# Score matmuls of sliding-window attention: 64 queries against 192 keys in place of 128 against 256

## The chip, the cores and the metric

The kernel runs on one core of a Trainium2 chip. The metric is the time of one execution in microseconds on the device, as the median of several runs. TensorE (PE in the profile) multiplies matrices, with weight loads (PEld) as instructions of their own; VectorE (DVE), ScalarE (ACT) and GpSimd (POOL) work on tiles in on-chip memory; SyncE (SP) issues most of the transfers.

## The reference

One layer of a decoder trunk for 1024 prompt tokens and 8 x 4 decode tokens. The part that matters here is the attention of the prompt: 8 query heads of 64 channels share 2 key heads, and a query sees the 128 newest keys including its own, with a learned sink in the softmax's denominator. The reference works in blocks of 128 queries and takes 256 keys for each, the block before and the block itself; the mask leaves 128 of them.

```python
a = jnp.arange(WINDOW)[:, None]
c = jnp.arange(2 * WINDOW)[None, :]
d = a + WINDOW - c
mask = (d >= 0)[None] & (d < WINDOW)[None] & (blk * WINDOW + c[None] - WINDOW >= 0)
...
s = jnp.einsum('bnqhgd,bnkhd->bnhgqk', q, k).astype(jnp.float32) * (HEAD_DIM ** -0.5)
s = jnp.where(mask[None, :, None, None], s, -jnp.inf)
m = jnp.maximum(jnp.max(s, axis=-1, keepdims=True), sink)
p = jnp.exp(s - m)
denom = jnp.sum(p, axis=-1, keepdims=True) + jnp.exp(sink - m)
w = (p / denom).astype(v.dtype)
return jnp.einsum('bnhgqk,bnkhd->bnqhgd', w, v)
```

Around it stand an RMS norm, one input projection, a pooling mixer, an output projection, a SwiGLU FFN and a gated per-layer input.

## The kernel before, in words

All activations lie with channels on partitions. The 1056 tokens are cut into three groups of 352. Most of the time goes into the projections and the FFN, whose weights are split into a high and a low part (L173 casts on ScalarE, L174 subtracts on VectorE), with three matmuls of one pass for each product. The attention's own matmuls are in full fp32, and each of them has two records in the profile. All matmuls go through the helper at L128, all transposes through the one at L122.

The eight blocks of the prompt are worked through in the order 6, 7, 5, 0, 1, 2, 3, 4. A step of the loop issues, in this order: `scores` of the next block, one `filler` (a projection's matmuls, 12 or 24 of 352 columns), `turned` of the current block, another `filler`, and `values` of the current block. The scores of blocks 6 and 7 are issued ahead of the loop, among the decode tokens' attention. TensorE keeps this written order throughout. On VectorE and ScalarE the framework's scheduler decides the order, except where `fix` pins an instruction.

`scores(b)` multiplies, for each pair of heads c and each key head kv, the 128 queries of the block (weights of 64 rows, 128 columns) with 256 keys; kv 0 lies on the lower 64 rows and kv 1 on the upper. Four PSUM banks hold the result, two heads each. Query q of a block sees the key in column c of the block before where c > q, and column c of its own block where c <= q, so exactly one of the two blocks counts for each c. The kernel packs them into a tile `t` of 128 columns a head: ScalarE copies the previous block's 128 scores (L749), and VectorE's predicated copy (L750) puts the own block's scores over them where the mask says so. Block 0 has no block before it; its scores get a mask added instead (L752).

`weigh` is the softmax over the packed tile, once for each key head: maximum (L696), scale and sink (L698, L700), the exponentials with their sums on ScalarE (L707), the denominator (L712, L713), and the division on GpSimd (L715). `turned` transposes the weights, four heads into a bank, and VectorE multiplies each bank with two masks (L771 for the part that belongs to the own block or to the mixed tile `vmix`, L773 for the rest). `values` multiplies these with the value tiles: four matmuls of 128 rows x 64 columns that need the L771 products, and four of 64 x 64 that need those of L773. `put` splits the result into high and low parts (L686, L687).

The fillers bring their own work to the other engines: L856, L875, L877, L885 and L862 to L866 evict, add and square the projections' results.

Of the kernel before, what the change touches and what calls it, by code (L numbers as in the profile page):

```python
# [16 lines left out]
P = 128  # L17
# [14 lines left out]
WIN = 128  # L32
# [13 lines left out]
NEG = -1.0e30  # L46
# [16 lines left out]
def trunk_kernel(  # L63
# [33 lines left out]
    te, ve, se, ge = nc.tensor, nc.vector, nc.scalar, nc.gpsimd  # L97
# [10 lines left out]
    def nm(s):  # L108
        cnt[0] += 1
        return f"{s}{cnt[0]}"  # L110

    def act_tile(shape, dt=F32, s="a"):
        return apool.tile(shape, dt, tag="a", bufs=A_SLOTS, name=nm(s))
# [12 lines left out]
    def mm(*args, **kw):  # L126

        ins = te.matmul(*args, **kw)  # L128
        if pinned[0]:
            tc.keep_in_program_order(ins)  # L130

    def bank():
        return psum.tile([P, 512], F32, tag="b", name=nm("b"))
# [363 lines left out]
    n = 4 * NDEC * PST  # L497
# [141 lines left out]
    kT, vT, qT = qkv[0], qkv[1], qkv[2:]  # L639
# [5 lines left out]
    qd, am, vdec = misc[:, 0, :], misc[:, 1:5, :], misc[: NDEC * DSEQ, 5, :]  # L645
    for c in range(4):
        n = NDEC * DSEQ
# [69 lines left out]
    def m4(i):  # L717
        return am[:, i, :].unsqueeze(1).to_broadcast([P, 4, WIN])
# [4 lines left out]
    def scores(b, now_=True):  # L723


        t = act_tile([P, 8, WIN])
        nk = 2 * WIN if b else WIN
        lo = b * WIN + WIN - nk
        at = WIN * 4 // nk
        both = [[bank() for _ in range(4 // at)] for _ in range(2)]  # L730
        for c in range(4):
            for kv in range(2):
                rows = slice(64 * kv, 64 * kv + 64)
                i = c % at
                mm(
                    both[kv][c // at][:, i * nk : (i + 1) * nk],
                    qT[c][rows, b * WIN : (b + 1) * WIN],
                    kT[rows, lo : lo + nk],
                    start=True,
                    stop=True,  # L740
                )
        for kv in range(2):
            tk = t[:, 4 * kv : 4 * kv + 4, :]
            for i, ps in enumerate(both[kv]):
                tc_ = tk[:, i * at : (i + 1) * at, :]
                v = ps.rearrange("p (c k) -> p c k", k=nk)
                if b:
                    m = am[:, 0, :].unsqueeze(1).to_broadcast([P, at, WIN])
                    se.copy(tc_, v[:, :, :WIN])  # L749
                    ve.copy_predicated(tc_, m.bitcast(mybir.dt.int32), v[:, :, WIN:])  # L750
                else:
                    ve.tensor_tensor(tc_, v, m4(1), op=ALU.add)  # L752
        if now_:
            weigh(t)
        return t

    def weigh(t):
        for kv in range(2):
            hs = slice(4 * kv, 4 * kv + 4)
            softmax((t[:, hs, :], 4, skp[:, hs], nskp[:, hs]))  # L760
# [144 lines left out]
    td = dscores()  # L905
    fixed[0] = False
    t = scores(order[0], False)
    project(5, WQ[-1], 1)
    filler(1)
# [4 lines left out]
    weigh(t)  # L914
    filler(1)
    ahead = scores(order[1])
    dvalues(pts, od)
    put(od, SEQ, NDEC * DSEQ)
# [6 lines left out]
    for a, b in zip(order, order[1:] + [None]):  # L925

        fixed[0] = lazy[0] = b is None
        t2 = ahead or (None if b is None else scores(b))
        ahead = None
        filler(1)  # L930
        parts = turned(a, t)
        if b is None:
            lazy[0] = False
            weights(WOA[1][0], 1)
        filler(1)
        values(a, parts)
        t = t2
# [488 lines left out]
def _layout(i):  # L1426

    f = lambda a: np.asarray(a, dtype=np.float32) if not isinstance(a, np.ndarray) else a
    i = {k: f(v) for k, v in i.items()}
    tok = lambda a, s, c: np.concatenate([a.reshape(-1, c), s.reshape(-1, c)]).reshape(T, c // P, P).transpose(2, 1, 0)  # L1430
    heads = np.concatenate([np.r_[64 * c : 64 * c + 64, 64 * (4 + c) : 64 * (4 + c) + 64] for c in range(4)])
    w_in = i["w_in"][0]
    w_in = w_in[:, np.r_[512:768, heads, 768:1280]]
    w_out = i["w_out"][0][np.r_[heads, 512:1024]]
    tiles = lambda w: w.reshape(w.shape[0] // P, P, w.shape[1] // P, P).transpose(2, 1, 0, 3)
    wd = i["w_down"][0]
    gains = np.stack([i[n][0].reshape(KC, P).T for n in ("norm_mix_pre", "norm_mix_post", "norm_ffn_pre", "norm_ffn_post")], 1)
    sinks = i["attn_sinks"][0]
    q, c = np.arange(WIN)[:, None], np.arange(WIN)[None, :]
    masks = np.stack([1.0 * (c <= q), np.where(c <= q, 0.0, NEG), 1.0 * ((q <= c) | ((q >= 64) & (c < 64))), 1.0 * (q > c)], 1)  # L1440
    r = np.arange(P)[:, None]
    rb, rj = (r % 32) // DSEQ, r % DSEQ
    kb, kw = np.arange(NDEC * WIN)[None, :] // WIN, np.arange(NDEC * WIN)[None, :] % WIN
    nb, nj = np.arange(NDEC * DSEQ)[None, :] // DSEQ, np.arange(NDEC * DSEQ)[None, :] % DSEQ
    dmask = np.concatenate([(rb == kb) & (kw > rj), (rb == nb) & (nj <= rj)], 1)
    pfix = np.stack([np.maximum(w / (np.arange(16) + 1.0), 1.0) for w in PW])
    out = {
        "x": tok(i["x_prompt"], i["x_sample"], D),
        "p": tok(i["p_prompt"], i["p_sample"], PLE),
        "w_in": tiles(w_in),  # L1450
        "w_out_a": w_out[:, :512].reshape(2, 4, P, 2, 256).transpose(0, 3, 2, 1, 4),
        "w_out_b": tiles(w_out[:, 512:]),
        "w_pool": i["w_pool"][0].transpose(1, 0, 2),
        "w_gu": np.stack([tiles(i["w_gate"][0]), tiles(i["w_up"][0])], 1),
        "w_dn": wd[: SLAB * NSLAB * P].reshape(NSLAB, SLAB, P, 2, 2, 2, P).transpose(0, 4, 3, 2, 1, 5, 6).reshape(NSLAB, 2, 2, P, KC, P),
        "w_dl": wd[SLAB * NSLAB * P :].reshape(REST, P, 2, 512).transpose(2, 1, 0, 3),
        "w_pg": tiles(i["w_ple_gate"][0]),
        "w_ple": i["w_ple"][0].reshape(2, P, 4, 256).transpose(2, 1, 0, 3),
        "gains": gains,
        "pscale": i["pool_scale"][0].reshape(4, P).T,  # L1460
        "sink_p": np.broadcast_to(sinks, (P, 8)),
        "sink_d": np.repeat(sinks.reshape(2, 4).T, 32, axis=0),
        "masks": masks.astype(np.float32),
        "dmask": np.where(dmask, 0.0, NEG).astype(np.float32),
        "pfix": np.broadcast_to(pfix, (P, 4, 16)).astype(np.float32),
        "ck": i["cache_k"][0].reshape(NDEC, WIN, P).transpose(2, 0, 1),
        "cv": i["cache_v"][0].reshape(NDEC, WIN, P).transpose(1, 0, 2),
        "st": i["state_pool"][0].reshape(NDEC, PST, 4, P).transpose(3, 2, 0, 1),
    }
    return {k: np.ascontiguousarray(v) for k, v in out.items()}  # L1470
# [29 lines left out]
```

## Time and profile before

| | |
|---|---|
| median of 3 runs | 1084.95 us (1084.91 to 1085.83) |
| profiled execution | 1084.32 us, its span 1082.5 us |
| TensorE busy | 1076.1 us, 99% |
| VectorE busy | 871.1 us, 80% |
| ScalarE busy | 512.6 us, 47% |
| GpSimd busy | 281.1 us, 26% |

The span is the stretch from the first to the last instruction of the profiled execution. A row of a timeline gives the start in us, the duration in us, engine, line, operation, tiles written and read, shapes and the number of instructions that the row merges; [idle before <-releaser] is added where the engine stood still. For a matmul, 64*128 64x256 means weights of 64 rows and 128 columns with 256 columns streamed. A row of groups ends in "busy us, mean ns of one | idle us before". A row of stretches gives the stretch, its length, then for each engine the busy time and the number of instructions, then the granted clock, the share of transfers and GB/s.

### The profile page before, as it was taken

Reading aid. Unit: us, or ns where it says so; the run is one execution under the profiler, and the core shown is the slowest. Engines: PE = TensorE matmul, PEld = TensorE weight load, DVE = VectorE, ACT = ScalarE, POOL = GpSimd, SP = SyncE. Lnnn points to the kernel's source line nnn. Section 1 sums busy time; section 2 is a strip of 40 time slices with the busy share of each in tenths; the row PEclk is TensorE's granted clock in tenths of the full one; section 3 lists DMA queues with packets and bytes.
Section 4 is the critical chain, followed back from the end, with each engine's and each line's share of the span. In section 5 each row is a group of like instructions: output and inputs, shape, how many; then the busy total and the mean of one; then the engine's idle time right before and its main releaser. Section 6 shows DMA issues by size and latency. Waiting matters only on the chain.

```text
span 1082.5 us, 17732 instructions
## 1 busy us (share of the span) xinstructions
PE 1076.1 (99%) x6867; PEld 1060.0 (98%) x6867; DVE 871.1 (80%) x1312; ACT 512.6 (47%) x877; POOL 281.1 (26%) x212
## 2 busy tenths in 40 slices
PE   9999999999999999999999999999999999999998
PEld 9999988899999999999999999999999999999998
DVE  6776478886878956796598898898899997969973
ACT  7423277774555533345543344343344365545531
POOL 0073032200000022536536435445442000022300
PEclk9999999999999999999999999999999999999999
DMA  8121311534553332322222222222234556454351
GB/s 298 59 72 39 119 52 40 192 139 143 189 185 132 136 117 79 132 79 78 78 80 78 78 79 78 86 71 81 95 113 149 183 180 234 172 211 133 126 204 60
DMA packets 43572, 131.27 MB, mean 121 GB/s; under 512 B 5060, under 2 KB 15588, under 8 KB 43488
## 3 DMA queue, kind: packets, MB, share of 16 engines
q1 hardware_dynamic: 42160, 128.38, 34.7%
q10 hardware_dynamic: 1328, 1.77, 0.5%
q8 instruction: 54, 0.88, 0.3%
q14 instruction: 30, 0.25, 0.1%
HBM read 114.25 MB, written 15.87 MB: 120 GB/s over the span
## 4 chain that ended last, share of the span: by engine, by line
PE 96%; DVE 2%; POOL 1%; issue 1%; DMA 0%; ACT 0%; SPq 0%; DVEq 0%; POOLq 0%; ACTq 0%
PE b L128 95%; PE b L122 1%; POOL wr L1073 1%; DMA xr<-in_x_dram 0%; DVE wl L174 0%; DVE sl L174 0%; DVE hp L174 0%; DVE hf L1148 0%; DVE ap L1243 0%; DVE w L174 0%; ACT sh L173 0%; DVE fl L174 0%; DVE p L1100 0%; DVE c L1100 0%; DVE u L1100 0%
## 5 line engine op out<-in xcount | busy, mean ns | idle before, releaser
L1073 POOL TENSOR_TENSOR wr<-wr,wr 128x512 f32<-128x512 f32 x108 | 171.9, 1606 | 482.5 <-DMA wr<-in_w_gu_dram 259.4
L173 ACT CAST wh<-wr 128x1024 fp32r<-128x1024 f32 (+1 forms) x138 | 142.1, 1031 | 163.6 <-PE b L128 92.5
L174 DVE TENSOR_TENSOR wl<-wr,wh 128x1024 fp32r<-128x1024 f32 (+1 forms) x138 | 168.8, 1225 | 48.2 <-ACT wh L173 31.7
L128 PE MATMUL b<-fh,wh 128*128 128x352 f32 x624 | 201.5, 323 | 0.0
L128 PE MATMUL b<-fl,wh 128*128 128x352 f32 x624 | 199.9, 320 | 0.0
L128 PE MATMUL b<-fh,wl 128*128 128x352 f32 x624 | 199.8, 320 | 0.0
L173 ACT CAST sh<-wr 128x1024 fp32r<-128x1024 f32 x72 | 75.7, 1052 | 137.1 <-POOL wr L1073 126.8
L128 PE MATMUL b<-fh,sh 128*128 128x352 f32 x416 | 134.3, 323 | 0.0
L128 PE MATMUL b<-fl,sh 128*128 128x352 f32 x416 | 133.2, 320 | 0.0
L128 PE MATMUL b<-fh,sl 128*128 128x352 f32 x416 | 133.2, 320 | 0.0
L174 DVE TENSOR_TENSOR sl<-wr,sh 128x1024 fp32r<-128x1024 f32 x72 | 97.6, 1358 | 36.8 <-PE b L128 19.1
L128 PEld LDWEIGHTS b<-fl,wh 128*128 128x128 f32 x624 | 117.3, 188 | 0.0
L128 PEld LDWEIGHTS b<-fh,wh 128*128 128x128 f32 x624 | 117.0, 188 | 0.0
L128 PEld LDWEIGHTS b<-fh,wl 128*128 128x128 f32 x624 | 116.9, 187 | 0.0
L128 PE MATMUL b<-h,wh 128*128 128x352 f32 x480 | 105.8, 327 | 0.3 <-ACT h L426 0.3
L128 PE MATMUL b<-hid,wh 128*128 128x352 f32 x416 | 99.4, 322 | 0.0
L128 PEld LDWEIGHTS b<-h,wh 128*128 128x128 f32 x480 | 82.8, 191 | 1.2 <-ACT h L426 0.6
L1073 POOL TENSOR_TENSOR wr<-wr 128x512 f32<-128x512 f32 x36 | 51.0, 1417 | 105.2 <-DVE w L174 105.2
L128 PEld LDWEIGHTS b<-fl,sh 128*128 128x128 f32 x416 | 78.2, 188 | 0.0
L128 PEld LDWEIGHTS b<-fh,sh 128*128 128x128 f32 x416 | 78.0, 188 | 0.0
L128 PEld LDWEIGHTS b<-fh,sl 128*128 128x128 f32 x416 | 77.9, 187 | 0.0
L128 PE MATMUL b<-hp,sh 128*128 128x352 f32 x320 | 76.5, 322 | 0.4 <-DVE ap L1243 0.3
(195 smaller groups left out, 2242.4 us busy)
## 6 DMA issues: line engine op xcount, KB each, us to landing
wr<-in_w_gu_dram SPq DMA_DIRECT2D x88, 512.0 KB, 3.3
wr<-in_w_dn_dram SPq DMA_DIRECT2D x40, 512.0 KB, 3.2
wr<-in_w_pg_dram SPq DMA_DIRECT2D x16, 512.0 KB, 3.6
x<-in_x_dram SPq DMA_DIRECT2D x6, 704.0 KB, 9.8
x1d<-x SPq DMA_DIRECT2D x6, 704.0 KB, 3.5
x<-x1d SPq DMA_DIRECT2D x6, 704.0 KB, 5.6
out_y_dram<-yo SPq DMA_DIRECT2D x24, 176.0 KB, 1.8
wr<-in_w_out_b_dram SPq DMA_DIRECT2D x8, 512.0 KB, 3.3
```

The lines of the kernel that those rows point to most:

```text
L122: ins = te.transpose(out, src, ident)
L128: ins = te.matmul(*args, **kw)
L173: fix(se.copy(hi, src))
L174: fix(ve.tensor_tensor(lo, src, hi.bitcast(F32), op=ALU.subtract))
L1073: ge.tensor_tensor(out, a, b, op=op)
```

## The change

Of the 256 keys of a block, a query q < 64 may use only keys 0 to 191 (previous block above q, own block up to q), and a query q >= 64 only keys 64 to 255. The change computes these alone: for blocks 1 to 7, each matmul of 128 queries and 256 keys becomes two of 64 queries and 192 keys. In a head's 256 PSUM columns, the first half's rows hold keys 0 to 191 in columns 64 to 255, the second half's hold keys 64 to 255 in columns 0 to 191. So columns 64 to 191 are, for the first half, the previous block, and for the second, the own block. ScalarE copies these 128 columns as the default, for all rows in one instruction as before. VectorE's predicated copy is made twice, for 64 partitions and 64 columns of two heads each: for the first half the own block's first 64 keys where c <= q, for the second the previous block's last 64 where c > q. The mask in DRAM changes to fit.

```diff
+        sides = [(0, WIN, 0, 0, nk)] if not b else [(0, 64, 64, 0, 192), (64, WIN, 0, 64, 192)]
         for c in range(4):
-            for kv in range(2):
-                rows = slice(64 * kv, 64 * kv + 64)
-                i = c % at
-                mm(
-                    both[kv][c // at][:, i * nk : (i + 1) * nk],
-                    qT[c][rows, b * WIN : (b + 1) * WIN],
-                    kT[rows, lo : lo + nk],
-                    start=True,
-                    stop=True,
-                )
+            i = c % at
+            for q0, q1, at0, k0, n in sides:
+                for kv in range(2):
+                    rows = slice(64 * kv, 64 * kv + 64)
+                    mm(
+                        both[kv][c // at][q0:q1, i * nk + at0 : i * nk + at0 + n],
+                        qT[c][rows, b * WIN + q0 : b * WIN + q1],
+                        kT[rows, lo + k0 : lo + k0 + n],
+                        start=True,
+                        stop=True,
+                    )
...
                 if b:
-                    m = am[:, 0, :].unsqueeze(1).to_broadcast([P, at, WIN])
-                    se.copy(tc_, v[:, :, :WIN])
-                    ve.copy_predicated(tc_, m.bitcast(mybir.dt.int32), v[:, :, WIN:])
+                    se.copy(tc_, v[:, :, 64:192])
+                    for rs, ks, at0 in ((slice(0, 64), slice(0, 64), 192), (slice(64, P), slice(64, P), 0)):
+                        m = am[rs, 0, ks].unsqueeze(1).to_broadcast([64, at, 64])
+                        ve.copy_predicated(tc_[rs, :, ks], m.bitcast(mybir.dt.int32), v[rs, :, at0 : at0 + 64])
...
-    masks = np.stack([1.0 * (c <= q), np.where(c <= q, 0.0, NEG), 1.0 * ((q <= c) | ((q >= 64) & (c < 64))), 1.0 * (q > c)], 1)
+    masks = np.stack([1.0 * np.where(q < 64, c <= q, c > q), np.where(c <= q, 0.0, NEG), 1.0 * ((q <= c) | ((q >= 64) & (c < 64))), 1.0 * (q > c)], 1)
```

TensorE, SyncE and GpSimd keep their order. The scheduler places some instructions of VectorE and ScalarE elsewhere. After the change, the lines below L728 have numbers higher by 3 (L750 is L753, L771 is L774, L773 is L776, L866 is L869; L749 is L750). In the order's rows `a` are activation tiles, `b` PSUM banks, `sm` and `es` the softmax's sums and sinks, `nmx` its maxima.

VectorE, at the products of block 6 while block 7's softmax runs (V1 of the prediction), before:

```order
L700 TENSOR_TENSOR es_1543<-c_75,nmx_1541 128x4
L698 SCALAR_TENSOR_TENSOR nmx_1556<-mx_1554,c_1289 128x4
L700 TENSOR_TENSOR es_1558<-c_75,nmx_1556 128x4
L771 TENSOR_TENSOR a_1611<-b_1613,a_1280 128x512
L773 TENSOR_TENSOR a_1612<-b_1613,a_1280 128x512
L712 TENSOR_TENSOR sm_1546<-sm_1546,es_1543 128x4
L771 TENSOR_TENSOR a_1611<-b_1620,a_1280 128x512
L713 RECIPROCAL sm_1546<-sm_1546 128x4
L773 TENSOR_TENSOR a_1612<-b_1620,a_1280 128x512
```

and after:

```order
L700 TENSOR_TENSOR es_1567<-c_75,nmx_1565 128x4
L698 SCALAR_TENSOR_TENSOR nmx_1580<-mx_1578,c_1289 128x4
L774 TENSOR_TENSOR a_1635<-b_1637,a_1280 128x512
L700 TENSOR_TENSOR es_1582<-c_75,nmx_1580 128x4
L776 TENSOR_TENSOR a_1636<-b_1637,a_1280 128x512
L774 TENSOR_TENSOR a_1635<-b_1644,a_1280 128x512
L712 TENSOR_TENSOR sm_1570<-sm_1570,es_1567 128x4
L776 TENSOR_TENSOR a_1636<-b_1644,a_1280 128x512
L713 RECIPROCAL sm_1570<-sm_1570 128x4
```

The second L774 (L771) now stands ahead of the softmax's sum L712.

VectorE, at the products of block 0 and the scores of block 2 (V4), before:

```order
L771 TENSOR_TENSOR a_1940<-b_1947,a_1280 128x512
L713 RECIPROCAL sm_1910<-sm_1910 128x4
L174 TENSOR_TENSOR wl_2082<-wr_1957,wh_2081 128x1024
L866 TENSOR_TENSOR acc_1301<-acc_1301,sq_1986 128x352
L687 TENSOR_TENSOR ml_1993<-b_1989,mh_1992 128x4x128
L750 COPY_PREDICATED a_1996<-a_1280,b_1997 128x256
L750 COPY_PREDICATED a_1996<-a_1280,b_1999 128x256
L750 COPY_PREDICATED a_1996<-a_1280,b_1998 128x256
L750 COPY_PREDICATED a_1996<-a_1280,b_2000 128x256
```

and after:

```order
L774 TENSOR_TENSOR a_1988<-b_1995,a_1280 128x512
L713 RECIPROCAL sm_1958<-sm_1958 128x4
L869 TENSOR_TENSOR acc_1301<-acc_1301,sq_2034 128x352
L687 TENSOR_TENSOR ml_2041<-b_2037,mh_2040 128x4x128
L174 TENSOR_TENSOR wl_2142<-wr_2005,wh_2141 128x1024
L753 COPY_PREDICATED a_2044<-a_1280,b_2045 64x2x64 x2
L753 COPY_PREDICATED a_2044<-a_1280,b_2046 64x2x64 x2
L753 COPY_PREDICATED a_2044<-a_1280,b_2047 64x2x64 x2
L753 COPY_PREDICATED a_2044<-a_1280,b_2048 64x2x64 x2
```

The weight split L174 now stands behind the addition of squares and the split L687 of block 0's values; on ScalarE the cast L173 that feeds it stands behind L686 in the same way. Each predicated copy has become two.

## The prediction

> **What bounds the kernel now.** I read the page first: busy times, the chain that ended last.
>
> ```profile
> span 1082.5 us, 17732 instructions
> ...
> PE 1076.1 (99%) x6867; PEld 1060.0 (98%) x6867; DVE 871.1 (80%) x1312; ACT 512.6 (47%) x877; POOL 281.1 (26%) x212
> ...
> PEclk9999999999999999999999999999999999999999
> ...
> PE 96%; DVE 2%; POOL 1%; issue 1%; DMA 0%; ACT 0%; SPq 0%; DVEq 0%; POOLq 0%; ACTq 0%
> ```
>
> TensorE is the bound, at the full clock throughout. So TensorE time saved counts in full, unless TensorE then has to wait for someone. Whether it has to is a question of the stage: attention lies at 129 to 219 us. One stretch there, and all that comes after (length, then busy TensorE, weight loads, VectorE, ScalarE, GpSimd):
>
> ```profile
> 188.94:200.75 11.81, 11.81 (x87) 9.98 (x85) 11.34 (x27) 8.44 (x34) 3.09 (x2) 1.00 0.26 90
> 220.00:1080.00 860.00, 857.99 (x5410) 857.13 (x5408) 712.66 (x980) 396.96 (x551) 222.88 (x144) 1.00 0.37 125
> ```
>
> From 188.94 to 200.75 VectorE is busy 11.34 of 11.81 us: only 0.47 us is idle. After 220 us TensorE is idle for 2 of 860 us, so what attention gains reaches the end. Next, where TensorE meets VectorE. Each block's value matmuls need the masked products of its turned weights, L771 and L773 of VectorE. I call the eight places V1 to V8, for blocks 6, 7, 5, 0, 1, 2, 3, 4. TensorE's rows there (rows of 32 records hold a block's value matmuls and the next block's scores):
>
> ```profile
> 153.47 3.99 PE L128 MATMUL b<-a,a 128*64 128x256 f32 x32
> 162.30 2.77 PE L128 MATMUL b<-a,a 128*64 128x256 f32 x32
> 169.90 3.83 PE L128 MATMUL b<-a,a 128*64 128x256 f32 x32
> 180.49 3.09 PE L128 MATMUL b<-a,a 128*64 128x512 f32 x20
> 190.37 3.60 PE L128 MATMUL b<-a,a 128*64 128x256 f32 x32
> 200.73 3.68 PE L128 MATMUL b<-a,a 128*64 128x256 f32 x32
> 211.16 1.68 PE L128 MATMUL b<-a,a 128*64 128x256 f32 x16
> 217.67 1.68 PE L128 MATMUL b<-a,a 128*64 128x256 f32 x16
> ```
>
> and the product that comes last for the first of them (the second key head's L771):
>
> ```profile
> 153.12 0.68 DVE L771 TENSOR_TENSOR a<-b,a 128x512 f32<-128x512 f32 x1
> 161.34 0.68 DVE L771 TENSOR_TENSOR a<-b,a 128x512 f32<-128x512 f32 x1
> 169.40 0.68 DVE L771 TENSOR_TENSOR a<-b,a 128x512 f32<-128x512 f32 x1
> 179.84 0.68 DVE L771 TENSOR_TENSOR a<-b,a 128x512 f32<-128x512 f32 x1
> 188.26 0.68 DVE L771 TENSOR_TENSOR a<-b,a 128x512 f32<-128x512 f32 x1
> 200.07 0.68 DVE L771 TENSOR_TENSOR a<-b,a 128x512 f32<-128x512 f32 x1
> 209.80 0.68 DVE L771 TENSOR_TENSOR a<-b,a 128x512 f32<-128x512 f32 x1
> 216.62 0.68 DVE L771 TENSOR_TENSOR a<-b,a 128x512 f32<-128x512 f32 x1
> ```
>
> Four rows are the same work (32 records, 256 columns): 3.60 us at V5, 3.68 at V6, 3.83 at V3, 3.99 at V1. V5's product ended at 188.94, 1.43 us ahead of need, so 3.60 is without a wait, and TensorE already waits 0.08 at V6, 0.23 at V3, 0.39 at V1. At V6 the product ends at 200.75, after TensorE's start at 200.73. The margin (start less product's end) is 0.28 at V2, none at V4 (180.52 against 180.49), 1.43 at V5, 0.68 at V7, 0.37 at V8, less 0.06 for the signal (at V6 the second head starts at 200.73 + 0.08, its product ended at 200.75). So in four of eight places TensorE is already at VectorE's pace.
>
> **The change part by part.** TensorE: seven blocks (not block 0) swap 8 matmuls of 64 rows x 128 weight columns and 256 keys for 16 of 64x64 and 192 keys.
>
> ```profile
> L128 PE MATMUL b<-a,a 64*128 64x256 f32 x112 | 14.0, 389 | 0.0
> L128 PE MATMUL b<-a,a 128*64 128x256 f32 x56 | 8.3, 392 | 0.0
> L128 PE MATMUL b<-a,a 64*64 64x256 f32 x56 | 4.6, 402 | 0.0
> L128 PE MATMUL b<-a,a 64*128 64x128 f32 x16 | 1.2, 285 | 0.0
> L128 PE MATMUL b<-a,a 128*64 128x16 f32 x32 | 1.1, 210 | 0.0
> ```
>
> Each matmul here has two records. Eight at 256 keys take 14.0/7 = 2.00 us; eight at 128 keys (block 0) 1.2; 192 keys lie halfway, 1.60. There are twice as many, but four run abreast where two did: four 64*64 matmuls of 256 columns take 4.6/7 = 0.66 us, four of 128*64 (two pairs in turn) 8.3/7 = 1.19. So 0.40 less a block, and 0.05 for the first load, which is of 64 columns (131 ns below, where loads of 128 columns take about 187). Seven times 0.45 is 3.2 us. Also, the scores of blocks 5, 2, 3 and 4 now follow value matmuls that already are 64*64, so a change of tile form falls away. The two rows of 64*128 put 128 columns at 0.8/8 = 0.10 a step, so 256 at some 0.21; V7's 1.68 us are six steps, five of them between its first and last start (1.05), and a tail of 0.39 (the mean duration), which leaves 0.24 for two first loads (0.05 each) and one change of form. I take 0.12 four times, 0.5 us. TensorE has 3.7 us less work. Nothing else of its queue moves.
>
> VectorE: 28 predicated copies of 128x256 become 56 of 64x(2x64), 128 elements a partition.
>
> ```profile
> L750 DVE COPY_PREDICATED a<-a,b 128x256 f32<-128x256 int32 x28 | 10.5, 440 | 0.9 <-ACT a L749 0.7
> L687 DVE TENSOR_TENSOR ml<-b,mh 128x256 fp32r<-128x256 f32 x13 | 5.0, 415 | 1.2 <-ACT mh L686 1.2
> L687 DVE TENSOR_TENSOR ml<-b,mh 128x128 fp32r<-128x128 f32 x3 | 0.9, 284 | 0.3 <-ACT mh L686 0.3
> ...
> 183.83 1.43 DVE L750 COPY_PREDICATED a<-a,b 128x256 f32<-128x256 int32 x4
> ```
>
> The new form is not in the trace. L687 drops from 415 to 284 ns when its elements go from 256 to 128, so half a predicated copy is 440 - 131 = 309 ns. Four in a row take 1.43, a spacing of (1.43 - 0.44)/3 = 0.33; less 0.13 makes 0.20, and eight take 7 x 0.20 + 0.31 = 1.71: 0.28 us more a block. Bounds: 0.17 each if only elements count (no increase), 0.33 each if a copy of half the size costs a whole one (1.3 us more a block); I take 0.20, nearest to the L687 rows. ScalarE's copy (L749) has the same size as before and costs nothing more. It can begin when half of a block's matmuls are done and the last one when all are, so some 0.25 and 0.45 us sooner after the scores' start; VectorE's last copy then ends about 0.2 us sooner after the scores' start, while TensorE is 0.45 to 0.57 us ahead. Each block thus narrows the margin by some 0.3 us, except where VectorE is queued behind other work: there it is 0.28 later outright.
>
> The order: at V1 the second L771 stood behind L712, which waited for ScalarE (0.20 in the row below); it now stands ahead and ends about 0.4 sooner. At block 1's products the weight split L174 now stands behind the square's addition and L687, and ScalarE's cast for it behind L686.
>
> ```profile
> 153.04 0.16 DVE L712 TENSOR_TENSOR sm<-sm,es 128x4 f32<-128x4 f32 x1 [0.20 <-ACT es L704]
> ...
> 181.64 1.24 DVE L174 TENSOR_TENSOR wl<-wr,wh 128x1024 fp32r<-128x1024 f32 x1 [1.03 <-ACT wh L173]
> 182.80 0.51 DVE L866 TENSOR_TENSOR acc<-acc,sq 128x352 f32<-128x352 f32 x1
> 183.23 0.68 DVE L687 TENSOR_TENSOR ml<-b,mh 128x512 fp32r<-128x512 f32 x1
> ...
> 180.58 1.03 ACT L173 CAST wh<-wr 128x1024 fp32r<-128x1024 f32 x1
> ...
> 182.30 0.58 ACT L686 CAST mh<-b 128x512 fp32r<-128x512 f32 x1
> ```
>
> The sum, as TensorE's lead over before at each place: the smaller of what TensorE wants and what VectorE allows. Block 6's scores save 0.45, lost at once, since the decode weights' transposes already wait for GpSimd:
>
> ```profile
> 139.25 0.92 PEld L122 LDWEIGHTS b<-c,a 128*128 128x128 f32 x9 [0.25 <-POOL a L715]
> ```
>
>  V1: 0.4 (the order). V2: wants 0.4 + 0.57, VectorE's product comes some 0.45 sooner (0.4 from V1, and a little from earlier scores); with the margin of 0.22 that makes 0.7. V3: 0.9, from the wait it had. V4: no margin, so VectorE's own shift, the 0.9 and some 0.3 because block 1's scores come sooner: 1.2. V5: wants 1.2 + 0.45. Its product: the cast for L174 now waits behind L686, which needs V4's matmuls. These ended about when the scores began (180.49 + 3.09 - 2.00 = 181.6); 1.2 sooner and with 0.6 for L686 that is 181.0, the cast (1.03) ends at 182.0, the split (1.24) at 183.3, the copies (1.71) at 185.0, against 183.83 + 1.43 = 185.26 before; the second L771 now also stands behind L712. The product ends some 0.1 sooner than at 188.94 and the lead is the margin, 1.4. V6: VectorE's stretch 188.94 to 200.75 has 0.47 idle; the product can come earlier by 0.1 (its start) + 0.47 - 0.28 = 0.3, or a little more if L174 and GpSimd collide less. I take 0.4: about 1.5 us of the lead are lost in a wait here. V7: wants 0.4 + 0.57; margin 0.63 and VectorE 0.2 sooner allow 0.8. V8: no scores lie between, its products follow TensorE's transposes, 0.8 stays. So 0.8 of 3.7 us is kept.
>
> The profiled execution took 1084.32 (span 1082.53); there the change makes 1083.5. The median of the runs is 0.63 above it, 1084.95, so I predict 1084.1.
>
> [...]
>
> **The rivals.**
>
> First, VectorE isn't the limit and TensorE keeps all of it: 1084.95 - 3.7 = 1081.2. For it: 96% of the chain is TensorE, and VectorE idles at several of the places. Against it: the waits at V1, V3, V4 and V6, and the 0.47 us at V6.
>
> Second, half a predicated copy costs a whole one, 0.33 us spacing: 0.13 x 8 = 1.07 more a block than I took. In the tight run of V5, V6 and V7, that is 3.2 us later, less the 0.8: 2.4 us slower, 1087.4. It decides from about 0.32 us per copy on. The L687 rows speak against it; that they are another operation leaves it open.
>
> Third, the loads don't overlap:
>
> ```profile
> L128 PEld LDWEIGHTS b<-a,a 64*64 64x64 f32 x56 | 1.5, 131 | 2.7 <-issue 2.7
> ```
>
> eight steps a block with 0.13 us exposed, 1.05 us; less 0.45 is 0.6 us more a block, 4.2 us in all, some of it in waits that exist: about 1088. The 64*64 and 16-column rows speak against it.
>
> Fourth, the same mechanism as mine with looser VectorE order: if the collision at V6 goes away (L174 took 1.62 at 193.18 against 1.24 at 181.64) the lead there may be 1.5, and the end 2.2 to 2.5 us faster, 1082.6.
>
> ```profile
> 193.18 1.62 DVE L174 TENSOR_TENSOR wl<-wr,wh 128x1024 fp32r<-128x1024 f32 x1 [0.36 <-PE b L128]
> ```
>
> **How the numbers follow.** Mine has 0.65, the first rival 0.13, the second 0.07, the third 0.03, the fourth 0.12. The bound of what can be told from no change is 0.2%, 2.2 us. Mine lies within it, and half of the fourth: same 0.71; faster 0.13 + 0.06 and a little of mine, 0.20; slower 0.09 with what is left of the second and third. The range: V6's lead between 0 and 2 gives 0.5 to 2.5 us at the end, a copy at 0.25 us would take the gain away, and the runs shown reach 0.9 above the median: 1082.0 to 1085.9. My own case alone is 1083.0 to 1085.3.
>
> **What would show it.** In the profile after: score matmuls as 64*64 64x192, 224 records, busy near 11 us instead of 14.0. Predicated copies x56 near 309 ns, eight in about 1.7. The row of value and score matmuls at V6, now shorter by its scores (3.60 less 0.57, 3.0 without a wait), longer by 1 to 2 us of waiting for L774, with the wait named in TensorE's loads; the windows before V6 with VectorE over 95% busy; V7's product just ahead of need. TensorE busy time hardly lower than its span. It is wrong if there is no wait at V6 (then the first or fourth rival), if copies take 0.4 us (second), or if a block's scores take 2 us or more (third).

## The result, and the profile after

The changed kernel takes 1090.82 us (median of 4 runs, 1090.36 to 1091.61), the kernel before 1085.39 us beside it (1084.91 to 1086.23). The ratio is 1.0053, with a 95% interval of 1.0039 to 1.0067: 5.4 us slower. I had forecast 1084.1, and 1085.9 as the upper end. The profiled execution took 1091.61 us. From its page, the span, the busy times, the clock and the chain that ended last:

```profile
span 1089.8 us, 17984 instructions
...
PE 1076.8 (99%) x6979; PEld 1057.9 (97%) x6979; DVE 880.5 (81%) x1340; ACT 512.6 (47%) x877; POOL 282.0 (26%) x212
...
PEclk9999999999999999999999999999999999999999
...
PE 89%; DVE 7%; ACT 2%; issue 1%; POOL 1%; DMA 1%; SPq 0%; ACTq 0%; DVEq 0%; POOLq 0%
```

TensorE's share of the chain falls from 96% to 89%, VectorE's rises from 2% to 7%. The granted clock was 0.91 in the first 20 us of this execution and 1.00 behind that, so in all of the attention. The stretch of attention, first before, then after (length, then busy TensorE, weight loads, VectorE, ScalarE, GpSimd):

```profile
125.00:235.00 110.00, 110.00 (x806) 95.56 (x805) 86.03 (x211) 74.61 (x254) 25.20 (x24) 1.00 0.32 109
```

```profile
125.00:235.00 110.00, 104.61 (x881) 88.24 (x880) 87.72 (x231) 70.68 (x247) 25.28 (x24) 1.00 0.31 106
```

TensorE had no idle time there, and now has 5.4 us of 110. What it waits for, from the waits of TensorE and of its weight loads in the same stretch (total, times, longest):

```profile
PE b L128 <- DVE a L774: 3.3, 6, 0.7
PE b L128 <- DVE es L700: 1.3, 2, 0.9
PE b L122 <- POOL a L715: 0.8, 1, 0.8
...
PEld b L128 <- DVE a L774: 6.8, 7, 1.2
```

L774 is the former L771, the masked products. L700, a short instruction of the softmax, stands directly behind the first key head's L774 in VectorE's order: at V6 that product ends at 205.74, L700 at 205.80, and the matmuls that need the product start at 205.88. So this row is a wait for VectorE too. The third lies ahead of V1, at the transposes of the decode tokens' attention. The timeline of TensorE shows the first: the value matmuls behind those that got through, at V1, V2, V4, V5, V6 and V7. V3 is one row, but of 3.56 us, where the prediction has 3.0 without a wait (3.60 less 0.57). V8 has no wait.

```profile
156.32 2.97 PE L128 MATMUL b<-a,a 128*64 128x256 f32 x46 [0.56 <-DVE a L774]
165.22 2.76 PE L128 MATMUL b<-a,a 128*64 128x256 f32 x30 [0.46 <-DVE a L774]
172.82 3.56 PE L128 MATMUL b<-a,a 128*64 128x256 f32 x48
...
184.54 2.53 PE L128 MATMUL b<-a,a 128*64 128x512 f32 x34 [0.31 <-DVE a L774]
195.04 2.97 PE L128 MATMUL b<-a,a 128*64 128x256 f32 x46 [0.59 <-DVE a L774]
207.22 2.97 PE L128 MATMUL b<-a,a 128*64 128x256 f32 x46 [0.72 <-DVE a L774]
218.21 1.67 PE L128 MATMUL b<-a,a 128*64 128x256 f32 x14 [0.65 <-DVE a L774]
224.72 1.68 PE L128 MATMUL b<-a,a 128*64 128x256 f32 x16
```

V8 starts at 224.72, 7.05 us later than before (217.67). 0.75 of this was there already when the first filler matmul after block 6's scores began (134.05 against 133.30), though these scores had become shorter: the program's first matmuls wait longer in this execution (1.4 us for L426, 0.3 before). So 6.3 us arise between there and V8.

The groups of instructions of the two edited operations:

```profile
L753 DVE COPY_PREDICATED a<-a,b 64x128 f32<-64x128 int32 x56 | 16.7, 301 | 1.0 <-ACT a L750 0.2
...
L128 PE MATMUL b<-a,a 64*64 64x192 f32 x224 | 10.5, 325 | 0.0
```

The matmuls came out as forecast, 10.5 us in place of 14.0. A predicated copy takes 301 ns, where I had 309. But the first number of a group is the time in which at least one of its instructions ran. 56 x 301 ns is 16.9, and the group has 16.7: these copies hardly overlap at all. Before, 28 x 440 ns made 12.3, and the group 10.5. VectorE's timeline, blocks 7, 5, 1, 2, 3 and 4 (start, length of all eight), and the softmax's maximum behind block 5's copies:

```profile
150.00 2.54 DVE L753 COPY_PREDICATED a<-a,b 64x128 f32<-64x128 int32 x8 [0.15 <-ACT a L750]
159.13 2.52 DVE L753 COPY_PREDICATED a<-a,b 64x128 f32<-64x128 int32 x8
161.68 1.28 DVE L696 TENSOR_REDUCE mx<-a 128x4 f32<-128x512 f32 x2
...
176.22 2.52 DVE L753 COPY_PREDICATED a<-a,b 64x128 f32<-64x128 int32 x8
188.35 2.52 DVE L753 COPY_PREDICATED a<-a,b 64x128 f32<-64x128 int32 x8
200.78 2.27 DVE L753 COPY_PREDICATED a<-a,b 64x128 f32<-64x128 int32 x8
211.52 2.53 DVE L753 COPY_PREDICATED a<-a,b 64x128 f32<-64x128 int32 x8
```

Eight copies take 2.52 us: a spacing of (2.52 - 0.30)/7 = 0.32 us, not 0.20. That is the spacing of the whole copies before (0.33), for half of the work. The row of block 3 is the odd one, 2.27. VectorE's order there differs:

```order
L753 COPY_PREDICATED a_2190<-a_1280,b_2191 64x2x64 x2
L753 COPY_PREDICATED a_2190<-a_1280,b_2193 64x2x64
L753 COPY_PREDICATED a_2190<-a_1280,b_2192 64x2x64 x2
L753 COPY_PREDICATED a_2190<-a_1280,b_2193 64x2x64
L753 COPY_PREDICATED a_2190<-a_1280,b_2194 64x2x64 x2
```

In the other blocks the two copies of a bank follow each other, on partitions 0 to 63 and then 64 to 127, so the start partition changes seven times among eight copies. Here the copies of one bank stand apart, the first next to another first and the second next to another second, so it changes five times; two steps became some 0.11 us shorter (the third and fourth copies start 0.21 us apart, and so do the fifth and sixth). That made the theory for the experiments: a copy that starts on another partition than the one before it waits until that one has ended (0.32 us apart, at 0.30 us each).

### The profile page after: what moved, and what is told of

Same layout as the page of the kernel before. It is cut to its first block, busy times and chain, and to the rows that moved or that the text cites. A ratio compares the mean times of both kernels' runs of the same rounds, so it can differ in the third digit from the quotient of the medians.

```text
span 1089.8 us, 17984 instructions
## 1 busy us (share of the span) xinstructions
PE 1076.8 (99%) x6979; PEld 1057.9 (97%) x6979; DVE 880.5 (81%) x1340; ACT 512.6 (47%) x877; POOL 282.0 (26%) x212
## 4 chain that ended last, share of the span: by engine, by line
PE 89%; DVE 7%; ACT 2%; issue 1%; POOL 1%; DMA 1%; SPq 0%; ACTq 0%; DVEq 0%; POOLq 0%
PE b L128 89%; DVE a L753 1%; ACT a L707 1%; DVE mx L696 1%; DVE wl L174 1%; DMA xr<-in_x_dram 1%; POOL wr L1076 0%; DVE sm L712 0%; DVE a L774 0%; DVE ml L687 0%; DVE a L776 0%; DVE a L821 0%; DVE sl L174 0%; DVE ap L1246 0%; PE b L122 0%
## 5 line engine op out<-in xcount | busy, mean ns | idle before, releaser
L173 ACT CAST wh<-wr 128x1024 fp32r<-128x1024 f32 (+1 forms) x138 | 142.0, 1031 | 157.8 <-PE b L128 94.5
L174 DVE TENSOR_TENSOR wl<-wr,wh 128x1024 fp32r<-128x1024 f32 (+1 forms) x138 | 168.4, 1222 | 44.6 <-ACT wh L173 29.1
L173 ACT CAST sh<-wr 128x1024 fp32r<-128x1024 f32 x72 | 75.7, 1052 | 139.7 <-POOL wr L1076 134.1
L174 DVE TENSOR_TENSOR sl<-wr,sh 128x1024 fp32r<-128x1024 f32 x72 | 97.1, 1351 | 36.4 <-ACT sh L173 23.5
```

The source lines that it names most:

```text
L173: fix(se.copy(hi, src))
L174: fix(ve.tensor_tensor(lo, src, hi.bitcast(F32), op=ALU.subtract))
```

## The experiments

Rival A was that half a copy costs a whole one wherever it starts, rival B that the 64x64 matmuls or the scheduler's other order make TensorE wait.

**One start partition.**

```diff
-for rs, ks, at0 in ((slice(0, 64), slice(0, 64), 192), (slice(64, P), slice(64, P), 0)):
+for rs, ks, at0 in ((slice(0, 64), slice(0, 64), 192), (slice(0, 64), slice(64, P), 64)):
```

> Both predicated copies of a bank work on partitions 0 to 63 (the second takes other PSUM columns), so that all copies start on the same partition; their number, their shape and the order on every engine are those of the changed kernel. The selection of the upper 64 queries is left out. Theory (a VectorE instruction whose tiles start on another partition than the last one's waits until that one has ended, and the two copies alternate between partitions 0 and 64): the copies now start about 0.20 us apart in place of 0.31, eight take about 1.7 us in place of 2.5, and the time is what I had forecast, 1084.5 (1083 to 1086). Rival A (a copy of half the size costs a whole one, 0.33 us, wherever it starts): still 0.31 apart, 1090.8. Rival B (64x64 matmuls or the scheduler's other order make TensorE wait, not the copies): copies 0.20 apart, yet 1089 to 1091.

Measured: 1084.38 us against 1085.05 before, ratio 0.9995 (0.9986 to 1.0004). The group, and block 5's copies with the maximum behind them:

```profile
L753 DVE COPY_PREDICATED a<-a,b 64x128 f32<-64x128 int32 x56 | 12.0, 286 | 0.1
...
155.89 1.67 DVE L753 COPY_PREDICATED a<-a,b 64x128 f32<-64x128 int32 x8
157.47 1.26 DVE L696 TENSOR_REDUCE mx<-a 128x4 f32<-128x512 f32 x2
```

56 x 286 ns is 16.0, the group 12.0: now they overlap. The spacing is (1.67 - 0.29)/7 = 0.20. From the first copy to the maximum it is 1.58 us, in the changed kernel 2.55: 0.97 us a block. With the same number, shape and order of instructions the whole loss is gone, so A and B fall. The interval of the ratio holds no change: this run can't be told from the kernel before. Of TensorE's shorter work little gets through, and the waits for the products that are left are at V3 and V6 (TensorE's weight loads in all, then TensorE's rows there):

```profile
PEld b L128 <- DVE a L774: 2.3, 3, 1.3
...
168.62 0.65 PE L128 MATMUL b<-a,a 128*64 128x256 f32 x2
169.52 2.97 PE L128 MATMUL b<-a,a 128*64 128x256 f32 x46 [0.26 <-DVE a L774]
...
199.16 0.62 PE L128 MATMUL b<-a,a 128*64 128x256 f32 x2
200.62 2.97 PE L128 MATMUL b<-a,a 128*64 128x256 f32 x46 [0.84 <-DVE a L774]
```

The longest, 1.3 us, is at V6, where I had put 1.5. From first start to end the value and score matmuls take 4.43 us at V6 and 3.87 at V3, some 1.4 and 0.9 above the 3.0 without a wait.

**Fewer changes of partition, with nothing left out.**

```diff
-                    for rs, ks, at0 in ((slice(0, 64), slice(0, 64), 192), (slice(64, P), slice(64, P), 0)):
-                        m = am[rs, 0, ks].unsqueeze(1).to_broadcast([64, at, 64])
-                        ve.copy_predicated(tc_[rs, :, ks], m.bitcast(mybir.dt.int32), v[rs, :, at0 : at0 + 64])
+                    later.append((tc_, v))
...
+        for rs, ks, at0 in ((slice(0, 64), slice(0, 64), 192), (slice(64, P), slice(64, P), 0)):
+            for tc_, v in later:
+                m = am[rs, 0, ks].unsqueeze(1).to_broadcast([64, at, 64])
+                tc.keep_in_program_order(ve.copy_predicated(tc_[rs, :, ks], m.bitcast(mybir.dt.int32), v[rs, :, at0 : at0 + 64]))
```

> The changed kernel with the predicated copies of a block in another order: first the four of partitions 0 to 63, then the four of 64 to 127, pinned so. Nothing is left out. Theory (alternating starts): one change of start partition in a block in place of seven, three quarters of the copies 0.20 us apart; since the first four follow ScalarE's copies (about 0.35 apart) and the other four come behind, a block's copies end after about 2.0 to 2.1 us in place of 2.5, so less than half of the lost 1.07 a block is left: about 1087.5 (1086 to 1089). Rival A (half a copy costs a whole one): 0.31 apart, 1090.8. Rival B (tiles or the scheduler's order): 1089 to 1091, since that is kept except for the pinned copies.

Measured: 1086.51 against 1085.05, ratio 1.0014 (1.0006 to 1.0023). VectorE's timeline, blocks 2 and 4:

```profile
185.91 1.82 DVE L758 COPY_PREDICATED a<-a,b 64x128 f32<-64x128 int32 x8
...
207.60 0.30 DVE L758 COPY_PREDICATED a<-a,b 64x128 f32<-64x128 int32 x1
208.15 1.63 DVE L758 COPY_PREDICATED a<-a,b 64x128 f32<-64x128 int32 x7 [0.25 <-ACT a L751]
```

Eight copies with one change take 1.82. In four of the seven blocks the second copy first waits for ScalarE (2.18 us from first to last at block 4), which I had counted. So most of the loss goes with the changes of partition while the whole change stays in place. With no change, one, five and seven, eight copies take 1.67, 1.82, 2.27 and 2.52 us: some 0.12 us a change.

**The copies alone.** The matmuls and the placing of the kernel before, each copy split in two:

```diff
                     se.copy(tc_, v[:, :, :WIN])
-                    ve.copy_predicated(tc_, m.bitcast(mybir.dt.int32), v[:, :, WIN:])
+                    for rs, ks in ((slice(0, 64), slice(0, 64)), (slice(64, P), slice(64, P))):
+                        m = am[rs, 0, ks].unsqueeze(1).to_broadcast([64, at, 64])
+                        ve.copy_predicated(tc_[rs, :, ks], m.bitcast(mybir.dt.int32), v[rs, :, WIN:][:, :, ks])
```

> The kernel before with its matmuls (128 queries, 256 keys) and with each predicated copy split in two, for partitions 0 to 63 and 64 to 127 and 64 columns of two heads, as in the change; the own block's scores outside these two squares are left out. Theory: the copies cost what they cost in the changed kernel (0.31 apart, eight in 2.5 us) and TensorE's gain is missing, so that the time is that of the changed kernel or above it: 1092 (1090 to 1095). Rival A: the same. Rival B (the 64x64 matmuls make the loss): near the kernel before, 1085.4 to 1087.

Measured: 1094.0 against 1085.05, ratio 1.0081 (1.0069 to 1.0094). Its groups:

```profile
L751 DVE COPY_PREDICATED a<-a,b 64x128 f32<-64x128 int32 x56 | 16.8, 301 | 1.6 <-ACT a L748 0.6
L128 PE MATMUL b<-a,a 64*128 64x256 f32 x112 | 14.3, 390 | 0.0
```

The copies cost what they cost in the change, without any 64x64 score matmul and in nearly the order of the kernel before. The loss is 8.9 us, 3 us above that of the change by the ratios, about what TensorE's shorter work is worth.

**The matmuls alone.** Two heads of a bank 192 columns apart, copies as before:

```diff
+            for c in (0, 2):
+                sides += [(c, 64, WIN, 0, 0, 256), (c + 1, 0, 64, 192, 0, 256)]
+                sides += [(c, 0, 64, 0, 0, 192), (c + 1, 64, WIN, 256, 64, 192)]
...
+                    vp, vo = (ps[:, j : j + 384].rearrange("p (c k) -> p c k", k=192)[:, :, :WIN] for j in (0, 128))
...
+                    se.copy(tc_, vp)
+                    ve.copy_predicated(tc_, m.bitcast(mybir.dt.int32), vo)
```

> The matmuls in 64 weight columns without the split copies: each bank holds two heads 192 columns apart, half of its matmuls take 192 keys and half 256, so that all columns that a copy of 128 partitions reads are written; ScalarE's and VectorE's copies are those of the kernel before (28 of 128x256). Nothing is left out. TensorE has some 0.28 us less a block and 0.5 for the change of tile form, 2.5 us in all. Theory: VectorE costs what it did before, so most of that gets through, less what is lost at the places that were at VectorE's pace already: 1.2 us faster than before (0.3 to 2.5), about 1083.9. Rival B (64x64 matmuls make the loss): 1088 or above.

Measured: 1083.92 against 1084.81, ratio 0.9993 (0.9985 to 1.0002). The interval holds no change; it excludes rival B, and a loss of over 0.2 us. My 1.2 us faster lies within it, but isn't shown by it.

**One copy a bank.**

```diff
-                    for rs, ks, at0 in ((slice(0, 64), slice(0, 64), 192), (slice(64, P), slice(64, P), 0)):
-                        m = am[rs, 0, ks].unsqueeze(1).to_broadcast([64, at, 64])
-                        ve.copy_predicated(tc_[rs, :, ks], m.bitcast(mybir.dt.int32), v[rs, :, at0 : at0 + 64])
+                    m = am[:, 0, 0:64].unsqueeze(1).to_broadcast([P, at, 64])
+                    ve.copy_predicated(tc_[:, :, 0:64], m.bitcast(mybir.dt.int32), v[:, :, 64:128])
```

> The changed kernel's matmuls, with one predicated copy of 128 partitions and 64 columns of two heads for each bank in place of the two of 64 partitions (the selection is wrong: the second half's is left out). Theory: four copies a block, all from partition 0, about 0.20 apart, some 0.9 us a block in place of 1.43 before and 2.5 after; VectorE then has time to spare and TensorE's shorter work (3.7 us) gets through for the most part: 1082.5 (1081.2 to 1084). Rival A (each copy costs 0.33 whatever its size): VectorE as before, 1083 to 1084.5. Rival B (64x64 matmuls or the scheduler's order): 1088 or above.

Measured: 1081.43 against 1085.05, ratio 0.9970 (0.9958 to 0.9981). With four copies a block and no change of partition, TensorE's gain gets through. What is wanted now is a version that needs one copy a bank and still selects rightly.

**That version.** The 128 rows of a bank are one half of the queries (`i`, which is also the bank) of two heads (`r`), in place of one head's two halves; `j` is the pair of heads and its place in the bank:

```diff
+        for i in range(2):
+            for j in range(2):
+                for r in range(2):
+                    for kv in range(2):
+                        rows = slice(64 * kv, 64 * kv + 64)
+                        o = both[kv][i][64 * r : 64 * r + 64, 256 * j : 256 * j + 192] if b else both[kv][0][64 * r : 64 * r + 64, (2 * i + j) * WIN : (2 * i + j + 1) * WIN]
+                        k0 = (b - 1) * WIN + 64 * i if b else 0
+                        q0 = b * WIN + 64 * i
+                        mm(
+                            o,
+                            qT[2 * j + r][rows, q0 : q0 + 64],
+                            kT[rows, k0 : k0 + (192 if b else WIN)],
+                            start=True,
+                            stop=True,
+                        )
...
+                ks, at0 = slice(64 * i, 64 * i + 64), 128 - 128 * i
+                se.copy(tc_, v[:, :, ks.start : ks.start + WIN])
+                ve.copy_predicated(tc_[:, :, ks], m.bitcast(mybir.dt.int32), v[:, :, at0 : at0 + 64])
```

> The change with another placing: the 128 rows of a bank are 64 queries of two heads (the lower 64 of both, or the upper 64 of both) in place of 128 queries of one head. A bank's rows then all want the same columns, and one predicated copy of 128 partitions and 64 columns of two heads does its selection, from partition 0: 28 copies in all, of the shape of the run with one copy a bank. Sinks, masks and the views behind are laid out to fit; nothing is left out. Theory: TensorE's work is that of the changed kernel, VectorE's that of the run with one copy a bank (four copies 0.20 apart, 0.9 us a block), so its time as well: 1081.5 (1080.5 to 1083), 3.5 us faster than before. What could go against it: three-level views in the mask products (L771, L773) that cost VectorE more than their 0.68 us; each 0.1 more would be 0.4 a block, and the time 1083 to 1084.

Measured: 1080.83 against 1084.81, ratio 0.9970 (0.9959 to 0.9981). It beats both kernels: 4.0 us by the medians, 3.3 by the ratio. Its groups (L775 is the former L771), block 2's copies, TensorE at V1, V3, V5 and V6, and the stretch of attention:

```profile
L775 DVE TENSOR_TENSOR a<-b,a 128x512 f32<-128x512 f32 x16 | 10.9, 681 | 0.7 <-PE b L122 0.7
L128 PE MATMUL b<-a,a 64*64 64x192 f32 x224 | 10.8, 326 | 0.0
L756 DVE COPY_PREDICATED a<-a,b 128x128 f32<-128x128 int32 x28 | 7.3, 297 | 0.3 <-ACT a L755 0.2
...
181.66 0.88 DVE L756 COPY_PREDICATED a<-a,b 128x128 f32<-128x128 int32 x4
...
152.83 3.34 PE L128 MATMUL b<-a,a 128*64 128x256 f32 x48
...
168.39 3.31 PE L128 MATMUL b<-a,a 128*64 128x256 f32 x48
...
187.74 2.98 PE L128 MATMUL b<-a,a 128*64 128x256 f32 x48
...
197.45 3.38 PE L128 MATMUL b<-a,a 128*64 128x256 f32 x48
...
125.00:235.00 110.00, 109.74 (x953) 96.95 (x953) 86.75 (x216) 77.88 (x259) 25.21 (x24) 1.00 0.32 111
```

A copy of 128 partitions and 128 elements takes 297 ns, as long as one of 64 partitions (286 to 301). Four take 0.88 in place of 1.43 before at blocks 2 and 3, and 1.10 to 1.20 in place of 1.44 to 1.65 at blocks 7, 5, 1 and 4. The mask products stay at 681 ns with three-level views. TensorE is busy for 109.74 of 110 us. V6 is one row again, but not without a wait: the same work takes 2.98 us at V5 and 0.36, 0.33 and 0.40 more at V1, V3 and V6. TensorE is still at VectorE's pace there: its weight loads wait three times for L775 in this stretch, 0.6 us in all, and the second key head's L775 ends 0.31 us after the row's start at V1 and 0.29 at V3, but 1.51 ahead of it at V5.

**Where the loss arises.** The changed kernel loses 6.3 us against the run with one start partition (1.0053 less 0.9995). I had priced the second rival by V5 to V7 alone, so two runs put the alternating starts into some blocks only:

```diff
-                    for rs, ks, at0 in ((slice(0, 64), slice(0, 64), 192), (slice(0, 64), slice(64, P), 64)):
+                    for rs, ks, at0 in ((slice(0, 64), slice(0, 64), 192), (slice(64, P), slice(64, P), 0) if b in (5, 6, 7, 1) else (slice(0, 64), slice(64, P), 64)):
```

> The run with copies from one start partition, but with the change's alternating starts in blocks 6, 7, 5 and 1 (the copies ahead of V1, V2 and V4); in blocks 2, 3 and 4 the upper half's selection is left out. The order on every engine is the changed kernel's. It asks where the 6.4 us arise that lie between that run and the changed kernel. As my second rival was priced (only the run of V5, V6 and V7 counts): no later than with one start, 1084.4 (to 1085.3). If each block's 1.07 us counts wherever TensorE is at VectorE's pace: blocks 7, 5 and 1 add up to 3.2 us, 1087.5 (1086.3 to 1088.5).

> The counterpart: alternating starts in blocks 2, 3 and 4 (the copies ahead of V5, V6 and V7), one start in blocks 6, 7, 5 and 1, where the upper half's selection is left out. As the rival was priced: all of the loss, up to the changed kernel's 1090.8 if the price was only too low (1087.4 by its own sum). If each block's 1.07 us counts: three blocks, 3.2 us more than with one start, 1087.6 (1086.5 to 1088.6), and the two runs' losses add up to the 6.4 us.

Measured: early blocks 1088.03 against 1084.63, ratio 1.0029 (1.0018 to 1.0040); late blocks 1087.06, ratio 1.0020 (1.0011 to 1.0029). Above the run with one start partition that is 3.7 and 2.7 us by the ratios, together 6.4; each ratio is known to about 0.1%, 1 us. Blocks 1 and 2 of the early run, and the weight loads' waits for the products, early and then late:

```profile
175.47 2.51 DVE L753 COPY_PREDICATED a<-a,b 64x128 f32<-64x128 int32 x8
187.59 1.67 DVE L753 COPY_PREDICATED a<-a,b 64x128 f32<-64x128 int32 x8
...
PEld b L128 <- DVE a L774: 4.8, 5, 1.3
```

```profile
PEld b L128 <- DVE a L774: 4.2, 5, 1.2
```

Both halves of the attention count: on average nearly one us for each block whose copies alternate, 3.7 for four early blocks and 2.7 for three late ones. Block 6, whose copies lie among the decode tokens' attention, counts too, though neither expectation had it: TensorE's wait for GpSimd's L715 ahead of V1 is 0.9 us in the early run and 0.4 in the late.

## Why the prediction was wrong, by its own steps

**The step that failed** is the spacing of the half predicated copy. I took 0.20 us from L687's drop from 415 to 284 ns, which is a drop of duration, of an instruction of 128 partitions, which starts on partition 0, and carried it over to a spacing. Its ends were 0.17 and 0.33, and the upper one held: 0.32. The number itself is right where the start doesn't change (0.20 with one start partition, 0.12 more for each change). What I left out, and so put at nothing, is that the start partition now changes with each copy. It cost eight copies 2.52 us in place of the 1.71 of the sum, and the maximum behind them began 0.97 us later than with one start. At block 3, a copy behind a change of start starts 0.01 to 0.02 us after the one before it has ended, and the two without a change start 0.09 us before that. So the spacing with a change, 0.32, is the copy's own 0.301 us and a little. Without one it is 0.20, at copies of 0.286.

**The second rival** named the right price of a copy, with its point of decision at 0.32, and got 0.07 of the chance, but its reason was wrong (half a copy costs a whole one; with one start it doesn't, 0.20 against 0.33). The sign that I had set for it, copies of 0.4 us, did not come: the copies got no longer, 301 ns, but further apart, so a sign in the spacing was needed. Its time, 1087.4, was too low, because it counted only the three blocks of the tight run V5 to V7 (and 0.13 x 8 is 1.04, not 1.07). The late blocks measured 2.7 us, near its 3.2, but the early ones, 6, 7, 5 and 1, cost another 3.7. I had myself written that TensorE was at VectorE's pace in four of eight places, three of them early; a later VectorE costs there at once. Six blocks at 0.97 us make 5.8 of the 6.3 us.

**What held.** TensorE's work: 10.5 us of score matmuls, forecast near 11, and with VectorE out of the way 3.3 to 4.0 us faster, forecast 3.7. The 0.7 us of waits that the prediction found in the kernel before at V1, V3 and V6 are no part of that: in the last version they are 1.1 us. Where neither kernel waits, at V5, the row went from 3.60 to 2.98 us, 0.62 less, forecast 0.57. The loads do overlap: a block's 32 score loads of 64x64 take 132 ns each, 4.2 us one after the other, and its score matmuls take 10.5/7 = 1.5 us, with no idle time before any, under the 2 that I had set as the sign. So the third rival is out. The duration of a half copy was 301 against 309 ns. With one start partition, that is with the spacing I had assumed, the time was 1084.38, 0.7 below the kernel before by the medians (forecast 0.8), though its interval holds no change. The largest wait was at V6, as I had named it, 1.3 us for 1.5; the one at V3, 0.9 by its row, I had not. So the mechanism, the gain lost to VectorE with the largest wait at V6, is the right account of a kernel that differs from this one in one number; that the sum came out so close is in part luck, as the waits were spread otherwise.

**The first rival**'s time came where the copies cost less than before, in the one-copy versions: 1081.43 and 1080.83 against its 1081.2. Its reason did not: VectorE still is the limit at V1, V3 and V6 in the second of them, by 0.33 to 0.40 us each, and in the first TensorE's loads wait twice for the product, 0.4 us in all. **The fourth** needed the weight split L174 to get shorter between V5 and V6. In the changed kernel both splits there got longer, where they took 1.19 and 1.62 us before:

```profile
195.56 1.85 DVE L174 TENSOR_TENSOR wl<-wr,wh 128x1024 fp32r<-128x1024 f32 x1
198.79 1.73 DVE L174 TENSOR_TENSOR wl<-wr,wh 128x1024 fp32r<-128x1024 f32 x1
```

With one start partition they took the same 1.85 and 1.73 us, so this is no part of the loss between the two runs, but it is 0.77 us more of VectorE's work ahead of the wait at V6 that is left. Why they got longer is not shown.

## What to carry to other kernels

When an instruction is split by partitions, look at the start partition of its neighbours: the two halves in turn lost the overlap that copies from one start partition have here, so half the work cost a whole spacing (0.32 us, 0.33 before, 0.20 from one start partition). Lay the data out so that all partitions of a tile want the same columns, or group the instructions by start partition. When an engine is later by a fixed amount each round, count every place at which another engine already keeps its pace, not only the tightest stretch.

## What the runs showed of the hardware that I had not expected

VectorE's predicated copies of 64x128 from PSUM start 0.20 us apart when all start on partition 0 and 0.32 when the start alternates between 0 and 64, at durations of 286 and 301 ns. It also holds the instruction behind them: the maximum L696, which starts on partition 0, began 1.58 us after the first of eight copies with one start partition and 2.55 with alternating ones, 0.97 later, of which the copies' own length explains 2.52 - 1.67 = 0.85. Mask, scores and tile all change their partitions together in these copies; which of the three decides was not taken apart. And copies of 128 partitions cost no more than those of 64 (297 ns against 286 to 301, 128 elements a partition in both).
